# Sixteen 32-byte runs written to the output as the first GpSimd transfer of a binary cross-entropy kernel

## The chip, the cores and the metric

One core of a Trainium2 chip. The metric is the device time of one execution in microseconds (us), median of several.

## The reference

```python
def setup_inputs():
    return {
        "pred": np.random.uniform(0.01, 0.99, (8192, 8192)).astype(np.float32),
        "target": np.random.randint(0, 2, (8192, 8192)).astype(np.float32),
    }

def reference(pred, target):
    eps = 1e-7
    pred = np.clip(pred, eps, 1 - eps)
    return -(target * np.log(pred) + (1 - target) * np.log(1 - pred))
```

The target is 0 or 1, so the result is -ln|target - 1 + pred|: one logarithm per element.

## The kernel before

The 67 million elements are cut into 37 chunks of up to 15360 columns by 128 partitions. Two rings in SBUF, the memory on the chip (pred in float32, target in bfloat16), hold two big chunks each. VectorE clips pred and adds target - 1 ("front"), ScalarE takes the absolute value and the logarithm, VectorE changes the sign ("back"), and the result is stored from the pred ring. The 16 DMA engines move the data between the memory of the device (HBM) and SBUF; GpSimd's queue issues almost every transfer; the cast of the target to bfloat16 is done by the transfer. The SP queue carries the first pred load and the last three stores.

```python
    warm = pool.tile([1, 8], fp32, name="warm", tag="warm")
    # ... cut: spot(ring, k, part) is chunk k's place in a ring
    def load(k):
        queue = nc.sync if k == 0 else nc.gpsimd
        nc.gpsimd.dma_start(out=spot(ring_t, k), in_=chunk(target, k))
        queue.dma_start(out=spot(ring_p, k), in_=chunk(pred, k))
    # ... cut: store, front, back
    with tc.manual_schedule():
        nc.vector.memset(warm, 1.0)
        for k in range(3):
            load(k)
        nc.scalar.activation(out=warm, in_=warm, func=Act.Ln)
        front(0)
        front(1)
        back(0)
        store(0)
        back(1)
        store(1)
        load(3)
        for k in range(2, n - 4):
            front(k, (0, 2))
            front(k, (1, 2))
            back(k, (0, 2))
            back(k, (1, 2))
            store(k)
            for j in range(k + 2, n if k == n - 5 else k + 3):
                load(j)
        # ... cut: the last four chunks
```

The little activation on `warm` is there to load the table of the logarithm early.

## Time and profile before

| what | before |
|---|---|
| time, median of 3 runs | 1865.96 us (1865.94 to 1866.08) |
| busy: VectorE, ScalarE, GpSimd | 60%, 48%, 3% |
| time taken by packets, of 16 DMA engines | 98.5% (GpSimd's queue) + 1.7% (SP's) |
| HBM traffic | 805.3 MB, 432 GB/s |
| one steady round (load, load, store) | 54.3 us |

In the lines of time order, the columns are start in us, duration in us, engine (a q after it means its sequencer or queue), source line, operation, what it writes and reads, and in brackets how long the engine idled before and what released it. A transfer "lands" when its last semaphore increment has arrived, the signal that its data are there. The lines themselves stand in the prediction below.

### The profile page before, as it was taken

The numbers are of one execution on the slowest core, as the hardware profiler recorded it, in microseconds if no ns is written. First come the engines' busy times: TensorE is split into PE (matmuls) and PEld (weight loads), VectorE is DVE, ScalarE is ACT, GpSimd is POOL, SyncE is SP. The second block draws the span as 40 slices with busy tenths as digits, with TensorE's granted clock in tenths as the row PEclk, the third lists the DMA queues.
The fourth block names the chain that finished last, engine by engine and source line by source line (L and its number), as shares of the span: only waits on it lengthen the run. The fifth ranks groups of instructions, "written<-read, shape, count | busy, mean of one in ns | idle before, by whom it ended". The sixth has DMA issues, their size and how long they took to land.

```text
span 1864.1 us, 619 instructions
## 1 busy us (share of the span) xinstructions
DVE 1122.2 (60%) x210; ACT 899.9 (48%) x142; POOL 57.5 (3%) x111
## 2 busy tenths in 40 slices
DVE  4655766555576655557665555766555576655585
ACT  3345553335555333555533355553335555333565
POOL 0000000000000000000000000000000000000000
DMA  9999999999999999999999999999999999999999
GB/s 295 374 357 341 353 343 368 383 384 351 347 352 344 371 382 384 348 349 353 347 367 384 382 352 347 353 345 368 385 382 352 345 353 348 365 387 380 353 334 389
DMA packets 15988, 671.13 MB, mean 360 GB/s; under 512 B 1776, under 2 KB 1776, under 8 KB 1904
## 3 DMA queue, kind: packets, MB, share of 16 engines
q0 software_dynamic: 15408, 658.25, 98.5%
q1 hardware_dynamic: 576, 12.85, 1.7%
q14 instruction: 4, 0.03, 0.0%
HBM read 536.87 MB, written 268.44 MB: 432 GB/s over the span
## 4 chain that ended last, share of the span: by engine, by line
DMA 35%; issue 26%; ACT 22%; DVE 15%; POOL 1%; DVEq 0%; POOLq 0%; PEldq 0%
DMA ring_p<-in_pred_dram 32%; ACT ring_p L88 11%; ACT ring_p L89 11%; DVE ring_p L85 7%; DVE ring_p L82 4%; DVE ring_p L93 4%; DMA out_dram<-ring_p 3%; POOL ring_t L73 0%; POOL out_dram L78 0%; DVEq L157 0%; POOL ring_p L74 0%; POOLq L78 0%; POOLq L73 0%; DVEq L82 0%; PEldq L157 0%
## 5 line engine op out<-in xcount | busy, mean ns | idle before, releaser
L88 ACT ACTIVATE ring_p<-ring_p 128x7680 f32<-128x7680 f32 (+1 forms) x70 | 450.6, 6437 | 941.4 <-DVE ring_p L85 941.4
L85 DVE SCALAR_TENSOR_TENSOR ring_p<-ring_t,ring_p 128x7680 f32<-128x7680 bf16 (+1 forms) x70 | 557.2, 7960 | 2.4
L82 DVE TENSOR_SCALAR ring_p<-ring_p 128x7680 f32<-128x7680 f32 (+1 forms) x70 | 284.0, 4057 | 399.0 <-DMA ring_p<-in_pred_dram 399.0
L93 DVE TENSOR_SCALAR ring_p<-ring_p 128x7680 f32<-128x7680 f32 (+1 forms) x69 | 284.0, 4117 | 321.5 <-ACT ring_p L89 321.5
L89 ACT ACTIVATE ring_p<-ring_p 128x7680 f32<-128x7680 f32 (+1 forms) x70 | 451.1, 6444 | 2.2
L74 POOL DMA_DIRECT2D ring_p<-in_pred_dram x36 | 19.3, 535 | 909.2 <-DMA out_dram<-ring_p 909.2
L78 POOL DMA_DIRECT2D out_dram<-ring_p x34 | 18.2, 537 | 851.0 <-DVE ring_p L93 851.0
L73 POOL DMA_DIRECT2D ring_t<-in_target_dram x37 | 20.3, 550 | 0.8 <-PEq L157 0.8
L99 ACT ACT_TABLE_LOAD x1 | 1.3, 1283 | 0.7 <-PEq L146 0.7
L96 DVE MEMSET warm<- 1x8 f32 x1 | 0.1, 65 | 0.8 <-PEq L146 0.8
L99 ACT ACTIVATE warm<-warm 1x8 f32<-1x8 f32 x1 | 0.2, 208 | 0.0
L146 POOL MEMSET const-float32-0.0<- 128x1 f32 x1 | 0.1, 98 | 0.2 <-issue 0.2
L146 POOL MEMSET const-bfloat16-1.0<- 128x1 bf16 x1 | 0.1, 101 | 0.0
L146 POOL MEMSET const-uint8-127<- 128x1 uint8 x1 | 0.1, 99 | 0.0
L146 POOL MEMSET const-float32-1.0<- 128x1 f32 x1 | 0.1, 98 | 0.0
## 6 DMA issues: line engine op xcount, KB each, us to landing
ring_p<-in_pred_dram POOLq DMA_DIRECT2D x32, 7680.0 KB, 35.9
out_dram<-ring_p POOLq DMA_DIRECT2D x32, 7680.0 KB, 29.2
ring_t<-in_target_dram POOLq DMA_DIRECT2D x32, 3840.0 KB, 46.8
ring_p<-in_pred_dram POOLq DMA_DIRECT2D x3, 3840.0 KB, 34.9
ring_t<-in_target_dram POOLq DMA_DIRECT2D x4, 1920.0 KB, 27.7
out_dram<-ring_p POOLq DMA_DIRECT2D x2, 3840.0 KB, 27.6
out_dram<-ring_p SPq DMA_DIRECT2D x2, 3840.0 KB, 15.7
ring_p<-in_pred_dram SPq DMA_DIRECT2D x1, 3840.0 KB, 18.8
```

Source lines behind the costliest of these rows:

```text
L73: nc.gpsimd.dma_start(out=spot(ring_t, k), in_=chunk(target, k))
L74: queue.dma_start(out=spot(ring_p, k), in_=chunk(pred, k))
L78: queue.dma_start(out=chunk(out, k), in_=spot(ring_p, k))
L82: nc.vector.tensor_scalar(out=p, in0=p, scalar1=EPS, scalar2=1 - EPS, op0=Alu.max, op1=Alu.min)
L85: nc.vector.scalar_tensor_tensor(out=p, in0=t, scalar=1.0, in1=p, op0=Alu.subtract, op1=Alu.add)
L88: nc.scalar.activation(out=p, in_=p, func=Act.Abs)
L89: nc.scalar.activation(out=p, in_=p, func=Act.Ln)
L93: nc.vector.tensor_scalar(out=p, in0=p, scalar1=-1.0, scalar2=None, op0=Alu.mult)
L96: nc.vector.memset(warm, 1.0)
L99: nc.scalar.activation(out=warm, in_=warm, func=Act.Ln)
L146: nc = _bacc.Bacc("TRN2", target_bir_lowering=False, num_devices=1)
```

## The change

The intent that can be read from the code is a first, tiny use of GpSimd's transfer path, spread over all 16 DMA engines, before the first real load. What it writes is overwritten by the store of chunk 0, so the result is the same.

```diff
-    warm = pool.tile([1, 8], fp32, name="warm", tag="warm")
+    warm = pool.tile([16, 8], fp32, name="warm", tag="warm")
 ...
     with tc.manual_schedule():
         nc.vector.memset(warm, 1.0)
+        nc.gpsimd.dma_start(out=chunk(out, 0)[0 : P : P // 16, : warm.shape[1]], in_=warm)
         for k in range(3):
             load(k)
```

## The prediction

> **What bounds the kernel now.** I read the page first (busy shares, slices, queues), then the groups of instructions by line, then the chain of waits, and last the order of time on GpSimd, which issues nearly all transfers. The page says at once that no compute engine is full, and that the DMA engines are, in every slice:
>
> ```profile
> span 1864.1 us, 619 instructions
> DVE 1122.2 (60%) x210; ACT 899.9 (48%) x142; POOL 57.5 (3%) x111
> DMA  9999999999999999999999999999999999999999
> q0 software_dynamic: 15408, 658.25, 98.5%
> q1 hardware_dynamic: 576, 12.85, 1.7%
> HBM read 536.87 MB, written 268.44 MB: 432 GB/s over the span
> ```
>
> The reader is to see 98.5% + 1.7% of the 16 engines' time taken by packets. The 432 GB/s counts the target at its 4 bytes in HBM; the smaller rate in the slices (360 on average) counts it at the 2 bytes that arrive after the cast. Next, what GpSimd does in the steady part, two rounds of it:
>
> ```profile
> 479.14 0.53 POOL L74 DMA_DIRECT2D ring_p<-in_pred_dram  x1 [28.45 <-DMA out_dram<-ring_p]
> 503.98 0.54 POOL L78 DMA_DIRECT2D out_dram<-ring_p  x1 [24.31 <-DVE ring_p L93]
> 504.50 0.55 POOL L73 DMA_DIRECT2D ring_t<-in_target_dram  x1
> 533.46 0.53 POOL L74 DMA_DIRECT2D ring_p<-in_pred_dram  x1 [28.41 <-DMA out_dram<-ring_p]
> ```
>
> One chunk of 15360 columns takes 533.46 - 479.14 = 54.32 us. It moves 128 x 15360 x 4 B = 7.864 MB three times (pred in, target in, result out), 23.59 MB, so 434.3 GB/s. The waits in this list are long, but they do not starve the DMA engines: in the stretch from 500 to 1700 us their share is 1.00, because the target load and the store are still in the queue when the next pred load is issued. VectorE and ScalarE idle behind it:
>
> ```profile
> L88 ACT ACTIVATE ring_p<-ring_p 128x7680 f32<-128x7680 f32 (+1 forms) x70 | 450.6, 6437 | 941.4 <-DVE ring_p L85 941.4
> L82 DVE TENSOR_SCALAR ring_p<-ring_p 128x7680 f32<-128x7680 f32 (+1 forms) x70 | 284.0, 4057 | 399.0 <-DMA ring_p<-in_pred_dram 399.0
> ```
>
> Last, the start, where the change sits:
>
> ```profile
> 0.73 1.28 ACT L99 ACT_TABLE_LOAD   x1 [0.73 <-PEq L146]
> 0.74 0.38 SPq L74 DMA_DIRECT2D ring_p<-in_pred_dram  x1
> 0.80 0.07 DVE L96 MEMSET warm<- 1x8 f32 x1 [0.80 <-PEq L146]
> 1.23 1.21 POOL L73 DMA_DIRECT2D ring_t<-in_target_dram  x2 [0.79 <-PEq L157]
> 2.03 0.21 ACT L99 ACTIVATE warm<-warm 1x8 f32<-1x8 f32 x1
> 2.41 0.56 POOL L74 DMA_DIRECT2D ring_p<-in_pred_dram  x1
> 19.53 4.16 DVE L82 TENSOR_SCALAR ring_p<-ring_p 128x7680 f32<-128x7680 f32 x1 [18.67 <-DMA ring_p<-in_pred_dram]
> 31.92 6.60 ACT L88 ACTIVATE ring_p<-ring_p 128x7680 f32<-128x7680 f32 x1 [29.69 <-DVE ring_p L85]
> ```
>
> The first pred load goes out on the SP queue at 0.74 us, before GpSimd issues anything, and ScalarE has no real work until 31.92 us.
>
> **What the Trainium skill says, and whether this trace agrees.** (1) "DMA: Bandwidth & Descriptors", section "Where 436 GB/s comes from": the fabric side tops out at 435.2 GB/s, while the HBM side would hold one core to about 358. The steady 434.3 GB/s sits on the first and well above the second, so the measurement decides for the fabric figure here. (2) Same page, "Why a DMA increments its semaphore by 16 and not by 1": a transfer is cut over the largest k up to 16 that divides the slowest dimension of both sides, so 16 rows give one run to each of the 16 engines; every GpSimd transfer also posts one semaphore increment per engine. The packet count agrees with the latter: 107 GpSimd transfers x (128 rows + 16 increments) = 15408. (3) Same page, "Anatomy of one DMA": some 2 us of fixed cost, mostly the receipt of the last write, and "Specifications": writes below 512 B are done as read-modify-write. No small data transfer is in the trace of before, so nothing there checks these. (4) Same page, "Issuing engines are not separate DMA queues": SP's and GpSimd's transfers share the 16 engines; the summed share of 100.2% above fits that.
>
> **The change part by part.** Nothing is removed. Added: one GpSimd transfer of 16 runs x 32 B = 512 B, from a tile widened from 1 to 16 partitions, into 16 places of the first output chunk (every eighth row of its 128), which the real store of chunk 0 overwrites later. The order of instructions shows what goes with it: the new transfer waits for the memset; the activation-table load now waits for the new transfer; the first store waits for it too; and every later GpSimd transfer takes the next of the eight completion semaphores in turn, so that each wait names a semaphore one higher, on the same transfers as before. No other instruction moves.
>
> Step 1, issue. The memset ends at 0.80 + 0.07 = 0.87 us, GpSimd starts issuing at 1.23, so the memset costs nothing. One issue is 0.54 to 0.60 us (1.21 / 2 at the start). Everything GpSimd issues at the start moves some 0.55 us later: first target load from 1.23 to about 1.8.
> Step 2, are the DMA engines idle in these 0.55 us? No: the SP's pred load of 3.93 MB is in their queue from about 1.1 us, and alone would fill them for 3.93 / 0.4343 = 9.1 us. They work on pred instead of on target, so the first clip may even start some tenths before 19.53. The sum up to the second chunk (four pieces of 3.93 MB, 36.2 us) does not change. Path: 0.
> Step 3, the DMA engines' own extra work: per engine one 32 B read and write and one semaphore packet. An ordinary chunk's row of 61440 B at the measured rate (27.1 GB/s per engine) takes 2.26 us, and 32 B would be 1 ns; the cost is overhead. My estimate, from the skill's 2 us fixed cost of which most is waiting for a receipt and little is occupation, is 0.1 to 0.5 us per engine. As the engines are full from here to the end, this part is paid in full: +0.3 us.
> Step 4, ScalarE. The small transfer should land within about 2 to 5 us of its issue (behind first packets of about 1.1 us each, 30720 B at that rate). The table load then ends before about 8 us even if it takes twice its 1.28 us, against work at 31.92. Path: 0, with over 20 us to spare.
> Step 5, the first store waits for a transfer that landed over 50 us before (store at 56.76). 0.
> Step 6, semaphores shifted by one of eight. The waits are for the same transfers. 0.
>
> Sum: 1865.96 + 0.3, and another 0.1 for a changed order of packets among the queues: 1866.4 us.
>
> **The rivals.** (a) The issue delay is paid in full, because the whole chain of GpSimd issues slides: +0.55, 1866.5 to 1866.8 with step 3. For it: the chain starts with the GpSimd's first issues. Against: the store and load waits later in the chain are waits for full engines, which have stored-up work. Hardly told from mine by the time alone. (b) The start phase. The rounds from pred load to pred load are not even at first: 96.16, 150.74, 206.32, 260.87, 315.73 give 54.58, 55.58, 54.55, 54.86 us, before they settle near 54.3 to 54.4. About 2 us are lost there in how loads, stores and engines fall in with each other. A shift at the start can win some of that back or lose as much again: 1864.5 to 1868.5. (c) A gain from having every engine's software ring used once before the first load. Against: the first target issues take 1.21 / 2 = 0.6 us, hardly longer than the later 0.55, and the engines are at work from 1.1 us. It would save under 0.5 us: 1865.5. (d) A lasting penalty: each later transfer's descriptors stand two places further in the rings; if a fetch or a wrap then fell badly in every transfer, a 2% loss would take 37 us / 107 = 0.35 us per transfer. Against: each transfer puts 9 descriptors on an engine (8 rows and an increment), an odd number, so in before they already start at all small alignments, with rounds even to 0.1 us. I give it 2%, at 1900 us.
>
> **Range and chances.** All data at the steady 434.3 GB/s would be 805.3 MB / 434.3 = 1854.3 us; the time now is 11.7 us (0.6%) above that, start and end included. So faster by over 2% is out of reach short of a different rate: 0.01. Slower by over 2% needs (d): 0.02. Within 2%: 0.97. Three runs lay within 0.14 us, so the width is all rival (b): 1864.8 to 1868.4, with 1866.4 in it.
>
> **What would show it.** In the profile of the changed kernel: a GpSimd transfer to the output at about 1.2 us of some 0.55 us, and the first target issue at about 1.8 (step 1); the first clip at 19.0 to 19.8 and the second chunk's at 40.0 to 40.5 (step 2); 32 more packets in the software queue, 15440 (step 3); the table load at 3 to 7 us with ScalarE's first chunk still near 32 us (step 4); steady rounds of 54.3 to 54.4 us (step 6 and (d)). Rounds before 500 us whose sum differs from before by more than 1 us would speak for (b). Wrong altogether would be steady rounds longer than 54.6 us, DMA slices under 9, or a table load so late that ScalarE's first chunk moves.

## The result, and the profile after

| | before | changed |
|---|---|---|
| median of 6 runs | 1866.02 us | 1866.29 us |
| range | 1865.83 to 1866.71 | 1865.82 to 1866.98 |

The ratio is 1.0001, with a 95% interval of 0.9988 to 1.0014: the same. The interval is some 2.4 us wide on either side, so the time alone cannot say whether the predicted 0.4 us was right or was nothing.

From the page of the changed kernel: busy shares as before and the slices too, but for one digit of ScalarE's, 32 packets more in the software queue, one group that was not there (L99), and the table load, which now waits for it.

```profile
q0 software_dynamic: 15440, 658.25, 98.5%
...
L102 ACT ACT_TABLE_LOAD x1 | 1.3, 1283 | 8.5 <-DMA out_dram<-warm 8.5
L99 POOL DMA_DIRECT2D out_dram<-warm x1 | 0.6, 616 | 0.8 <-DVE warm L96 0.8
```

The start of the changed kernel in order of time:

```profile
0.74 0.38 SPq L74 DMA_DIRECT2D ring_p<-in_pred_dram  x1
1.29 0.62 POOL L99 DMA_DIRECT2D out_dram<-warm  x1 [0.84 <-DVE warm L96]
1.90 1.09 POOL L73 DMA_DIRECT2D ring_t<-in_target_dram  x2
8.47 1.28 ACT L102 ACT_TABLE_LOAD   x1 [8.47 <-DMA out_dram<-warm]
17.53 4.16 DVE L82 TENSOR_SCALAR ring_p<-ring_p 128x7680 f32<-128x7680 f32 x1 [16.67 <-DMA ring_p<-in_pred_dram]
22.14 8.16 DVE L85 SCALAR_TENSOR_TENSOR ring_p<-ring_t,ring_p 128x7680 f32<-128x7680 bf16 x1 [0.44 <-DMA ring_t<-in_target_dram]
30.33 6.60 ACT L88 ACTIVATE ring_p<-ring_p 128x7680 f32<-128x7680 f32 x1 [20.36 <-DVE ring_p L85]
40.28 4.16 DVE L82 TENSOR_SCALAR ring_p<-ring_p 128x7680 f32<-128x7680 f32 x1 [9.99 <-DMA ring_p<-in_pred_dram]
57.00 0.54 POOL L78 DMA_DIRECT2D out_dram<-ring_p  x1 [52.43 <-DVE ring_p L93]
```

The second chunk's clip and the first store before the change:

```profile
40.04 4.16 DVE L82 TENSOR_SCALAR ring_p<-ring_p 128x7680 f32<-128x7680 f32 x1 [8.15 <-DMA ring_p<-in_pred_dram]
56.76 0.54 POOL L78 DMA_DIRECT2D out_dram<-ring_p  x1 [52.73 <-DVE ring_p L93]
```

The reader is to see three things. The first target issue is 0.67 us later (1.90 for 1.23). The first clip is 2.00 us *earlier* (17.53 for 19.53). And by the second chunk both are gone but for 0.24 us: its clip starts at 40.28 for 40.04, and the first store at 57.00 for 56.76. The 0.24 us can't be put down to the small transfer: in the experiments below the same clip starts at 40.04 with two such transfers and at 39.96 with six, and between 39.86 and 40.13 where GpSimd sends none at the start (the run with twenty memsets aside). A shift of 2 us went in and came out within 40 us. Later, two of the rounds:

```profile
588.31 0.53 POOL L74 DMA_DIRECT2D ring_p<-in_pred_dram  x1 [28.42 <-DMA out_dram<-ring_p]
642.66 0.54 POOL L74 DMA_DIRECT2D ring_p<-in_pred_dram  x1 [28.41 <-DMA out_dram<-ring_p]
```

One round is 54.35 us, as before.

The trace also records every packet of the DMA engines. In these records, of the changed kernel, the columns are start and duration in ns (on the records' own clock), queue (0 GpSimd's, 1 SP's) and bytes; they are of several engines, in order of start, with a few lines taken from each of three places:

```
 start  took queue  bytes
 16094     9     0     32      the small transfer's data, between two pred rows
 16100  1138     1  30720
 17234     9     0      4      its semaphore increment, about 1140 ns later
 17240  1138     1  30720
 18374  1151     0  15360      only now the first target row
```

### The profile page after: what moved, and what is told of

Read it like the earlier page. It is cut to its first block, busy times and chain, and to the rows that moved or that the text cites. A ratio compares the mean times of both kernels' runs of the same rounds, so it can differ in the third digit from the quotient of the medians.

```text
span 1864.4 us, 622 instructions
## 1 busy us (share of the span) xinstructions
DVE 1122.2 (60%) x210; ACT 899.9 (48%) x142; POOL 58.0 (3%) x112
## 3 DMA queue, kind: packets, MB, share of 16 engines
q0 software_dynamic: 15440, 658.25, 98.5%
## 4 chain that ended last, share of the span: by engine, by line
DMA 35%; issue 26%; ACT 22%; DVE 15%; POOL 1%; DVEq 0%; POOLq 0%
DMA ring_p<-in_pred_dram 32%; ACT ring_p L88 11%; ACT ring_p L89 11%; DVE ring_p L85 7%; DVE ring_p L82 4%; DVE ring_p L93 4%; DMA out_dram<-ring_p 3%; POOL ring_t L73 0%; POOL out_dram L78 0%; DVEq L160 0%; POOL out_dram L99 0%; POOL ring_p L74 0%; POOLq L78 0%; DVE warm L96 0%; POOLq L73 0%
## 5 line engine op out<-in xcount | busy, mean ns | idle before, releaser
L99 POOL DMA_DIRECT2D out_dram<-warm x1 | 0.6, 616 | 0.8 <-DVE warm L96 0.8
```

Source lines behind the costliest of these rows:

```text
L99: nc.gpsimd.dma_start(out=chunk(out, 0)[0 : P : P // 16, : warm.shape[1]], in_=warm)
```

## The experiments

Two questions were left. Why does pred come 2 us earlier when GpSimd's issue moved by 0.67 us only? And is the change free because it costs nothing, or because something hides it, so that it would cost more elsewhere?

**Theory T (turns).** Each DMA engine takes packets in turn from SP's ring and from GpSimd's. In before, pred rows and target rows of chunk 0 alternate from GpSimd's first packet on. The small transfer is two packets per engine (data, semaphore), and each uses up one turn of GpSimd's ring, for which SP's ring sends one full pred row. The first target row comes two rows later, 2 x 1.14 = 2.3 us. **Rival D (delay):** the later issue does it. **Theory H (hidden while there is work):** a late GpSimd issue is free as long as the engines have the pred load to send, and paid after that; **rival P:** it is paid in full.

The delays are edits of the kernel before, all others of the changed kernel.

The packet records give one number per kernel that T is about. The times here count from the first packet of SP's queue and are means over the 16 engines; the clip's start is from the order of time.

```
kernel                         first target row   last pred row ends   first clip
before                              4.32 us            15.72 us          19.53
changed                             6.59               13.43             17.53
two small transfers                 8.87               11.16             15.02
six small transfers                10.01                9.96             12.82
one transfer of 32 runs             6.57               13.42             17.34
same transfer, ScalarE's queue      4.26               15.69             19.43
delay alone, 0.50 us                4.90               15.17             19.60
```

### First delay: a memset instead of the transfer

```diff
         nc.vector.memset(warm, 1.0)
+        nc.gpsimd.memset(idle, 1.0)        # idle: [128, 512] float32, used by nothing else
```

> The kernel before, with the small transfer replaced by a GpSimd memset of 512 columns ahead of the first target load (work of GpSimd that sends nothing; estimated 0.3 to 0.7 us). Theory T (turns: each of the 16 engines takes one packet in turn from the SP ring and from the GpSimd ring, and the small transfer's two packets, data and semaphore, use up two turns of the GpSimd ring, each worth one pred row of 1.14 us): without packets there is nothing to use up, so the first clip stays near before's 19.53 us, 18.2 to 19.8. Rival D (the 0.6 us delay of the issue itself brings pred forward): first clip near 17.5 as in the changed kernel. Both: time within 1 us of before.

```profile
0.73 0.52 POOL L98 MEMSET idle<- 128x512 f32 x1 [0.29 <-POOLq L148]
1.26 1.21 POOL L74 DMA_DIRECT2D ring_t<-in_target_dram  x2
```

Inconclusive: the memset lay in time in which GpSimd would have waited anyway, and the target issue stayed at 1.26 us. The clip (19.44) and the time (1866.24 us, one run) are as before, as they must be when nothing was delayed.

### Second delay: a longer memset

The same with 1150 columns.

> The first delay was none: its memset ran from 0.73 to 1.25 us, in time that GpSimd has free anyway, and the target issue stayed at 1.26. This one is 1150 columns wide (0.52 us per 512 columns, so some 1.17 us) and should put the first target issue at 1.9 us, where the changed kernel has it, with no packet sent. T (turns): the first target row reaches the engines at most one turn later than in before, and the first clip lies at 18.2 to 19.6 us. Rival D (delay): 17.5 us as in the changed kernel. Time within 1 us of before.

```profile
1.73 1.21 POOL L74 DMA_DIRECT2D ring_t<-in_target_dram  x2
19.60 4.16 DVE L83 TENSOR_SCALAR ring_p<-ring_p 128x7680 f32<-128x7680 f32 x1 [18.74 <-DMA ring_p<-in_pred_dram]
```

The delay is 0.50 us (1.73 for 1.23; 1.9 was hoped for), three quarters of the changed kernel's 0.67, and the clip does not come forward at all: 19.60. D falls. In the table the first target rows do move, by 0.6 us on the average of the engines: followed from packet to packet (the records do not name the engine), half of the engines send one pred row more before target. But the clip waits for the slowest engine, which is among the other half. Time 1866.62 us in one run, 1866.65 for before.

### Two and six small transfers

```diff
-        nc.gpsimd.dma_start(out=chunk(out, 0)[0 : P : P // 16, : warm.shape[1]], in_=warm)
+        for i in range(2):     # and range(6)
+            nc.gpsimd.dma_start(out=chunk(out, 0)[i : P : P // 16, : warm.shape[1]], in_=warm)
```

> Two small transfers at the start, as the six, but two. T (a turn per packet): four packets per engine, four turns of 1.0 to 1.15 us, so the first clip moves by twice what one transfer moved it (19.53 to 17.53): 15.5 us, 15.0 to 16.1. If what counts is having any small transfer at all: 17.5. Time within 1 us of before.

> Six small transfers instead of one, each of 16 runs to other elements of chunk 0, all of them ahead of the first target load. T: 12 turns, more than the 5 or so pred rows that are left per engine once GpSimd's first packet comes, so pred has nothing of target ahead of it and the first clip falls to 11.5 to 14 us. D: the delay is 6 x 0.55 = 3.3 us and the clip falls about as far, so this run doesn't tell T from D; it tells both from a fixed effect (clip at 17.5 again). Cost in time: by the term on record (0.3 us of occupation per transfer) +1.8 us over before; by the packet records of the changed kernel (9 ns a packet) +0.2 us or nothing that shows.

Two transfers:

```profile
1.29 1.11 POOL L100 DMA_DIRECT2D out_dram<-warm  x2 [0.84 <-DVE warm L96]
15.02 4.16 DVE L82 TENSOR_SCALAR ring_p<-ring_p 128x7680 f32<-128x7680 f32 x1 [14.16 <-DMA ring_p<-in_pred_dram]
```

Six transfers:

```profile
8.33 0.54 POOL L74 DMA_DIRECT2D ring_p<-in_pred_dram  x1 [2.94 <-DMA out_dram<-warm]
12.82 4.16 DVE L82 TENSOR_SCALAR ring_p<-ring_p 128x7680 f32<-128x7680 f32 x1 [11.96 <-DMA ring_p<-in_pred_dram]
```

The dose is read from the table: the last pred row ends at 15.72, 13.43, 11.16 us with none, one and two transfers, so 2.29 and 2.27 us per transfer, two rows of 1.14 each. With six, pred goes out undisturbed in 9.96 us (10.00 with the long delay below) and there is nothing more to win. The run with six shows something further: GpSimd now has to wait for a small transfer's landing before it may issue the second pred load, because the eight semaphores that tell of landings come round again, and that issue moves from 2.41 to 8.33 us. The time does not move: 1866.14 us for 1866.05, ratio 1.0001 (0.9984 to 1.0017); with two, 1865.91 in one run. The term would have made six cost 1.8 us; the interval is wider than that, so this run does not settle the term.

### One transfer of 32 runs

```diff
-    warm = pool.tile([16, 8], fp32, name="warm", tag="warm")
+    warm = pool.tile([32, 8], fp32, name="warm", tag="warm")
 ...
-        nc.gpsimd.dma_start(out=chunk(out, 0)[0 : P : P // 16, : warm.shape[1]], in_=warm)
+        nc.gpsimd.dma_start(out=chunk(out, 0)[0 : P : P // 32, : warm.shape[1]], in_=warm)
```

> One small transfer of 32 runs of 32 B instead of 16, so two data packets and one semaphore packet per engine. T (every data run takes a turn of its own): three turns, first clip at 16.5 us, 16.1 to 16.9. Rival G (runs of one transfer on one engine share a turn, or a transfer takes a fixed two): 17.5 us. Time within 1 us of before.

```profile
17.34 4.16 DVE L82 TENSOR_SCALAR ring_p<-ring_p 128x7680 f32<-128x7680 f32 x1 [16.48 <-DMA ring_p<-in_pred_dram]
```

Here T in the form that I had written down is wrong and G is right. The packet records say why: there are 16 data packets of 64 B (11 ns each), not 32 of 32 B. The two short runs of one engine went as one packet. A turn belongs to a packet, not to a run; T stands with that word changed. Time 1866.46 us in one run.

### The same transfer from ScalarE's queue

```diff
-        nc.gpsimd.dma_start(out=chunk(out, 0)[0 : P : P // 16, : warm.shape[1]], in_=warm)
+        nc.scalar.dma_start(out=chunk(out, 0)[0 : P : P // 16, : warm.shape[1]], in_=warm)
```

> The same small transfer, issued by ScalarE's queue instead of GpSimd's. T: its two packets then use turns of another ring; the GpSimd ring's turns start with the first target row as in before, so the first clip is back at 18.8 to 19.8 us. Rival F (any small transfer at the start changes the order of the packets so that pred comes forward): first clip near 17.5. Time within 1 us of before in both.

```profile
0.89 0.38 ACTq L99 DMA_DIRECT2D out_dram<-warm  x1
19.43 4.16 DVE L82 TENSOR_SCALAR ring_p<-ring_p 128x7680 f32<-128x7680 f32 x1 [18.57 <-DMA ring_p<-in_pred_dram]
```

The transfer is the same, the clip is back at 19.43. So it is not a small transfer as such that brings pred forward but the turns that it uses in GpSimd's ring; F falls. Time 1866.56 us in one run.

### The small transfer with nothing else in the engines

```diff
     def load(k):
-        queue = nc.sync if k == 0 else nc.gpsimd
+        queue = nc.gpsimd
```

> The changed kernel with the first pred load moved from the SP queue to the GpSimd queue behind the first target load, so that nothing is in the engines when the small transfer comes. T: its landing, 7.1 us in the changed kernel, is mostly turns spent behind pred rows; alone it lands in 2 to 4 us. Rival W (short writes to HBM are slow themselves, or the software path is): 6 us or more. First clip at 19 to 21 us, time within 1.5 us of before.

```profile
3.02 1.28 ACT L102 ACT_TABLE_LOAD   x1 [3.02 <-DMA out_dram<-warm]
23.07 4.16 DVE L82 TENSOR_SCALAR ring_p<-ring_p 128x7680 f32<-128x7680 f32 x1 [22.21 <-DMA ring_p<-in_pred_dram]
```

The transfer lands 1.7 us after its issue, against 7.1 in the changed kernel: the other 5.4 us were spent behind pred rows, and W (short writes, or the path, are slow) falls. Of the 1.7 us, 1.2 pass before the first data packet starts (2.47 us from the span's start), and 0.4 from the last semaphore packet (2.62) to the landing (3.02). Two side results. The clip at 23.07 misses the expected 19 to 21: with both loads in one ring, in order, all 8 target rows go ahead of the 8 pred rows. And the engines' first large packet comes 1.41 us later than in the changed kernel (13.53 for 12.12 on the records' clock); the profiled span is 1865.7 us for 1864.4, the single time 1867.83 us, over all seven runs of before beside it (1865.60 to 1866.88). That looks as if a late *start of the engines* were paid one for one, unlike a late GpSimd issue; but it is one run of unknown state, and its first loads also go in another order, so it is not shown here. The long delay below is the firmer evidence that idle engines are paid for.

### A long delay and a medium one

```diff
+        for _ in range(20):      # and range(6)
+            nc.gpsimd.memset(idle, 1.0)    # idle: [128, 1024] float32
```

> Twenty memsets of 1024 columns ahead of the first target load: issue at about 0.73 + 20 x 1.05 = 21.7 us, target's first rows at about 23.6 (2 us after the issue, as the small transfer that ran alone had it). The pred load alone, 8 rows of 1.17 us per engine from 2.6 us on, is out at about 12.0. Theory H (a late GpSimd issue is free as long as the engines have the pred load to work on, and is paid one for one after that): 23.6 - 12.0 = 11.6 us idle, so +11.6 us over before, +10 to +13. Rival P (a late issue is paid in full): +20.5. Rival S (slack somewhere later takes it up): 0 to +3.

> The delay alone, as with twenty memsets, but with six, of 1.2 us each as measured there: target issue at about 7.9 us instead of 1.23, first target rows at about 10.2 (2.2 us after the issue), while the pred rows alone last to about 12.6. H (free while the engines have pred to work on): time within 0.6 us of before, first clip at 12.6 to 13.5. Rival P (a late issue is paid in full): +6.7 us.

Twenty memsets:

```profile
0.73 24.00 POOL L99 MEMSET idle<- 128x1024 f32 x20 [0.29 <-POOLq L149]
12.57 4.21 DVE L83 TENSOR_SCALAR ring_p<-ring_p 128x7680 f32<-128x7680 f32 x1 [11.72 <-DMA ring_p<-in_pred_dram]
24.67 1.21 POOL L74 DMA_DIRECT2D ring_t<-in_target_dram  x2
36.95 8.16 DVE L86 SCALAR_TENSOR_TENSOR ring_p<-ring_t,ring_p 128x7680 f32<-128x7680 bf16 x1 [20.17 <-DMA ring_t<-in_target_dram]
```

Six memsets:

```profile
6.67 1.21 POOL L74 DMA_DIRECT2D ring_t<-in_target_dram  x2
15.09 4.16 DVE L83 TENSOR_SCALAR ring_p<-ring_p 128x7680 f32<-128x7680 f32 x1 [14.23 <-DMA ring_p<-in_pred_dram]
```

With twenty the time is 1881.89 us for 1866.65 of before, ratio 1.0081 (1.0066 to 1.0096), so +15.2 us (12.3 to 17.9). That is outside the range that I had written for H (10 to 13), since the memsets took 24.0 us and not 21. (Nineteen took 0.95 us each. One took 4.84: it started at 12.83 us, the clip began at 12.57 and ended at 16.78, and the memset ended 0.89 us after that. The Trainium skill, "SBUF — State Buffer", section "Who interferes with whom", has VectorE's two-port modes and GpSimd lock each other out for a whole instruction, and these times fit that; which mode the clip ran in no run shows.) With the times that did occur, H can be checked without the guess: in the packet records the last pred row ends 10.0 us after the first and the first target row starts at 24.6, on the average of the engines, so they stood idle for 14.6 us. Of a delay of 23.44 us (24.67 - 1.23), 15.2 was paid. P (all of it) and S (little or none) fall.

With six, the issue is 5.44 us late (6.67 for 1.23) and the time is 1866.13 us for 1866.19, ratio 0.9998 (0.9981 to 1.0014): free, as H has it. P would pay the 5.4 us, which lies outside the interval (-3.5 to +2.6 us). The clip missed its range (15.09 for 12.6 to 13.5), this time because the memsets were faster (1.0 us each) than I had set them: in the packet records a target row still goes before the last pred row on seven engines, and before the semaphore packet that follows it on all of them.

### Five small transfers in every round

```diff
             store(k)
+            for i in range(5):
+                nc.gpsimd.dma_start(out=chunk(out, k + 1)[i : P : P // 16, : warm.shape[1]], in_=warm)
```

and none at the start. A second kernel has `warm` as [16, 128], so that the runs have 512 B.

> No transfer at the start; five in each of the 31 rounds instead, behind the store, each of 16 runs of 32 B to elements of the next chunk that its store overwrites: 155 transfers where the engines are full. By the term on record (0.3 us of every engine per transfer) +46 us, by its range of 0.1 to 0.5 +15 to +78. By the packet records (two packets of 9 ns, some 14 ns with the gap each): 155 x 0.028 = +4.3 us at most, likely +1 to +5. Rival R (positions in the descriptor rings matter): rounds uneven, some over 55 us.

> As the run with five per round, but runs of 512 B instead of 32 B. At the 27 GB/s of one engine 512 B are 19 ns, so by the packet records +1.5 us more than with 32 B. If short writes are dear (read-modify-write), this run is faster than the one with 32 B, or the same in spite of 16 times the bytes.

Runs of 32 B:

```profile
534.07 0.53 POOL L74 DMA_DIRECT2D ring_p<-in_pred_dram  x1 [26.32 <-DMA out_dram<-warm]
...
559.17 2.41 POOL L116 DMA_DIRECT2D out_dram<-warm  x5
...
588.48 0.53 POOL L74 DMA_DIRECT2D ring_p<-in_pred_dram  x1 [26.34 <-DMA out_dram<-warm]
```

Runs of 512 B:

```profile
534.76 0.54 POOL L74 DMA_DIRECT2D ring_p<-in_pred_dram  x1 [26.41 <-DMA out_dram<-warm]
...
589.25 0.54 POOL L74 DMA_DIRECT2D ring_p<-in_pred_dram  x1 [26.42 <-DMA out_dram<-warm]
```

This is the run that sizes the cost. With 155 transfers of 32 B the time is 1868.15 us for 1866.65, ratio 1.0009 (0.9994 to 1.0024): a cost of more than 4.5 us is excluded, where the term asked for 46 and the lower end of its range for 15. The rounds say it more finely: 54.41 us (588.48 - 534.07) for 54.35 in the changed kernel, so 0.06 us for five transfers, some 12 ns each (nearly all rounds from 480 us on lie at 54.37 to 54.43, against 54.32 to 54.37 in the changed kernel). That is between the records' 9 ns for the data packet alone and the 18 ns of data and semaphore packet together; how part of the 18 ns is hidden was not tested. R (positions in the rings) is seen in one place: the round that starts at 860.52 us took 57.3 us and the next 51.5, nothing lost in sum. GpSimd idled there before the pred load, the last 3.5 us of it for nothing that the profile shows. The run with 512 B has the same pair at the same round (57.4 and 51.6, from 861.73 us), and no other kernel of this case has such a wait, so it goes with something that these two share, the number of transfers before it among others; what it waits for is not shown.

With 512 B the round is 54.49, 0.14 us over 54.35 or some 28 ns per transfer, and the records have 27 ns for such a packet. So the shorter write is also the cheaper one, and that short writes are dear is refuted for what an engine pays here. But the time, 1876.31 us, ratio 1.0071 (1.0041 to 1.01), is 9.7 us over before, and 155 x 0.028 = 4.3 us is all that the even rounds explain. From about 1020 us on its rounds are uneven, 54.4 to 55.5. The expectation (+1.5 us over the 32 B kernel) was wrong by this, I did not find the cause, and one of its four runs took 1886.97 us. It stays open, and nothing above rests on it.

## Why the prediction was right

The predicted 1866.4 us stands against 1866.29, and its main reason, that the DMA engines have work while GpSimd is late, was shown by experiment. Point by point:

- Step 1 (issue): right in kind. The small transfer went out at 1.29 us, and target 0.67 us later, for the 0.55 predicted.
- Step 2 (engines not idle, path 0): right, and shown by the delays: 5.44 us of lateness free, and of 23.44 us only 15.2 paid, against 14.6 us of idle engines. The pred load reached the engines at 1.75 us and alone took 10.0 us, for the 1.1 and 9.1 reckoned, which changes nothing. Rival (a) of the prediction, that the delay is paid in full, falls with it. But the clip "some tenths" early was wrong: it was 2.00 us, outside the stated 19.0 to 19.8, because the step reckoned with time and not with turns. The second clip at 40.28 is inside its 40.0 to 40.5, since the order of the packets changed and not their sum.
- Step 3 (cost in the engines): the packets came out as counted, 15440, but the term was mis-sized. For the 0.3 us (0.1 to 0.5) the rounds show about 0.012 us per transfer. The reasoning took part of a landing time for time in which an engine is occupied; and the 2 us that it started from, with most of them waiting for a receipt, were not found so: alone the transfer landed in 1.7 us, and most of that (1.2 us) passed before its data packet. The total was not hurt, as 0.3 us is below what the runs can resolve; that the medians differ by 0.27 us, so near to the predicted 0.4, is luck and no support for that figure.
- Step 4 (ScalarE): path 0 is right. The landing was 7.1 us for the 2 to 5 predicted and the table load came at 8.47 for 3 to 7, since two turns behind other rows were not counted. ScalarE's first chunk did move, from 31.92 to 30.33 us, but earlier, and with the clip, not because of the table load.
- Steps 5 and 6 (first store, semaphores shifted by one): nothing seen, rounds of 54.32 to 54.37 us from 590 us on.
- Rival (b) (the start phase): the seven rounds between the pred loads at 96.86 and 479.03 us sum to 382.17 us for 382.98 before, a difference of 0.81, below the 1 us named as its sign, and one later round took 54.92 us. The run of the first delay, in which nothing was sent or delayed, has such rounds too: 382.54 us over the same seven, and one of 54.93 from 750.68 us on. So this wobble is there without the change. Rival (c), a gain, and rival (d), a lasting penalty in every transfer, were not seen; the wobble leaves a gain of some tenths untestable.
- One reading needs a correction. The prediction set 434.3 GB/s against the fabric's 435.2 and let the measurement decide for the fabric. But 434.3 counts the target at its 4 bytes in HBM; what crosses on the SBUF side is 362 GB/s (500 to 1700 us). In the packet records a target row of 30720 B in SBUF takes 2281 ns and a pred row of 61440 B 2267 ns, so an engine's time goes with the elements, or with the wider side, and not with the bytes in SBUF. That the engines are full stands; that the ports to SBUF fill them is not shown.

## What to carry to other kernels

Where the DMA engines set the time, ask of every added transfer how long an engine is occupied (here 12 ns) and not how long it takes to land (1.7 to 7.1 us); and ask of every later issue whether the engines run dry before it, not how late it is. Two queues that feed the same engines share them by packets, so, as here, a packet of 4 bytes can hand the other queue a row of 30720: order loads by counting packets in each queue. And a start that is reshuffled by 2 us buys nothing when the sum of bytes ahead of the next bottleneck is unchanged.

## What the Trainium skill lacked or had wrong

- "DMA: Bandwidth & Descriptors", section "Where 436 GB/s comes from", lets the HBM side (about 358 GB/s) bind transfers between HBM and SBUF, though the same note calls a measured 425 GB/s near the fabric's rate. Here one core, running alone, kept 23.59 MB of HBM traffic per 54.35 us, 434 GB/s, in the steady part, two thirds of it reads, with 362 GB/s on the SBUF side.
- The same page, section "Queues, rings and completion order", states the turns by packet, and the runs agree. It lacks that in these records every row of 15360 to 61440 B is a packet, and the semaphore increment one too, with a turn of its own: one small transfer let the other ring ahead by 2.29 us, two rows and not one.
- The same page, section "Specifications", has the DMA engines do a read-modify-write below 512 B. In what an engine is occupied nothing of it showed: 9 ns for 32 B, 27 ns for 512 B.
